# Two hybrid layers on one core: modulation vectors from feature-major weights, and a first stage built around them

## The chip, the cores and the metric

The kernel runs on one core of one Trainium2 chip. The metric is the device time of one execution in microseconds (us). Five engines work in parallel, each through its own list of instructions: TensorE (PE in the profile, its weight loads PEld), VectorE (DVE), ScalarE (ACT), GpSimd (POOL) and SyncE (SP), which here issues the transfers (DMAs) from device memory.

## The reference

256 tokens of width 1024 pass two layers. In each, the condition vector c makes six vectors of 1024, which shift, scale and gate the activations. Cut to this:

```python
def rmsnorm(x, g):
    return x * lax.rsqrt(jnp.mean(x * x, axis=-1, keepdims=True) + EPS) * g

mod = c_act @ ada_w + ada_b                  # c_act = silu(c), ada_w 1024 x 6144
sh1, sc1, gt1, sh2, sc2, gt2 = [m[:, None, :] for m in jnp.split(mod, 6, axis=-1)]

h = rmsnorm(x, mix_pre_g) * (1.0 + sc1) + sh1
proj = h @ w_in                              # 1024 x 10272: z, xbc, dt, sc_b, sc_c, sc_h, gates
...                                          # Mamba-2 scan, short convolution, gates -> mix
x = x + gt1 * rmsnorm(mix, mix_post_g)
h = rmsnorm(x, ffn_pre_g) * (1.0 + sc2) + sh2
u = causal_dwconv(h @ w_up, ffn_conv_w, ffn_conv_b)
u_gate, u_val = jnp.split(u, 2, axis=-1)
f = (jax.nn.silu(u_gate) * u_val) @ w_down
x = x + gt2 * rmsnorm(f, ffn_post_g)
```

The second layer has attention (sparse and latent) in place of the scan and its own condition vector and weights `w_ada_2`; its six vectors are called sha, sca, ga (around the attention) and shf, scf, gf (around its feed-forward part).

## The kernel before, in words

**The stream.** All weights are fp32 and are read once, some 230 MB. They come as half chunks of at most 128 x 1024 into six buffers `raw`. ACT makes `hi` of a half chunk (a rounded copy in the format that TensorE multiplies), VectorE makes `lo` = raw - hi, five buffers each. An activation is split the same way (`hh` and `hl` for h, `h3h` and `h3l` for h3, and so on), and a product is three: hi by xh, lo by xh, hi by xl. `cast_next` takes the next half chunk of the list `keys` and issues its cast and difference; u16 means half chunk number 16 of the list. The first 16 (`w0`, 128x768 and 128x800 for each slice) belong to the first stage, u16 to u23 to the z part of `w_in`.

**The order.** Everything is put in order when the program is built. `_Order` keeps a clock for each engine and a rank for each task (tasks are generators); `O.spawn` starts one, `O.drain` runs one to its end. SP issues the transfers in the order of `keys`. Every engine operation is issued in one helper, so all have line 401 in the profile; transfers have their own lines (510 `raw`, 784 `ada0`, 435 a row broadcast over the partitions).

**The modulation vectors.** gt1, gt2, ga and gf are wanted as rows (1024 values, the same in all partitions), the other six as columns (128 features in the partitions, 8 columns). Their weights come with 128 of the 1024 inputs in the partitions. `ada_mul` lets VectorE multiply each half chunk by a column of silu(c) (`cact`) and add it into one accumulator `adaacc`; `ada_task` then has TensorE sum it over the partitions against `ones`: eight products of width 1 for a column vector, two of width 512 (`row_sum`) for a row. `mix_in` puts these chunks between the others in `keys`. gt2, shf and gf go another way (`adp_load`, `adp_add`, `adp_fill`, `adp_end`): buffers of their own, 6 or 7 of their 8 parts on VectorE (`ND`), the rest as products of width 512 (`adp,cb` and `adp,ones`) in waits of TensorE. shf comes out as a row, and `adp_end` turns it into columns by eight products `ones,row`.

**The first stage.** Of the first layer, h is needed at once. Slice by slice (t = 0 to 7, 128 features each) `mod_acc` accumulates the shift and the scale on VectorE (`ada0acc`), `mod_sum` adds TensorE's part (`cact,ada0a`, and the sum against `ones`) and makes m, `mod_h` makes hf and hh on ACT, `mod_lo` makes hl, and `half(0)` and `half(1)` are the slice's 39 products with w0 (the columns B, C and a quarter of x of the scan's input, and dt). `cast0` casts one half chunk. POOL scales xT by the token's rsqrt for slices 1 to 7. After this stage come z (`z_task`), the rest of x, and so on.

**The tail of gt2.** `tail` is the code between two blocks: it makes the residual, norms it, turns it by products `btok,xr` (four rows of the list, two records each in the trace) and applies shift and scale, which gives h3h and h3l. While h3h is made, TensorE's list holds the products of the `fill` vector, here shf:

```python
    h, k_h, of = tail("gt2", True, "h3", "sca", "sha", "shf")
```

In the second layer the list of keys goes nc, ns, nw (attention's keys and values), then queries, then `wo2`, `up2`, `dn2`.

Of the kernel before, what the change touches and what calls it, by code (L numbers as in the profile page):

```python
# [15 lines left out]
D = 1024  # L16
# [9 lines left out]
           "shf": ("w_ada_2", 3), "scf": ("w_ada_2", 4)}  # L26


def _plan():
# [129 lines left out]
for _key, _n in PF_W.items():  # L159
# [6 lines left out]
         "gq": 256, "gks": 256, "gkw": 256, "mq": 128, "mk": 128}  # L166
# [8 lines left out]
def _rows(i):  # L175
    def swap(v):
# [8 lines left out]
         "mq": swap(i["mla_q_norm_2"][128:]), "mk": swap(i["mla_k_norm_2"][128:])}  # L185
# [221 lines left out]
def _body(ctx: ExitStack, tc: tile.TileContext, wst, pf_d, rows_d, cst_d, xT_d, x_d, w2_d, out_d):  # L407
# [353 lines left out]
    on_pe = ("gt2", "shf", "gf")  # L761
    assert sorted(map(str, keys)) == sorted(str(k) for k, _, _ in PLAN if k[0] != "ada0" and k[1] not in on_pe)
# [35 lines left out]
    AC.activation(cact, P("c", 0, 16), AF.Silu)  # L798
# [18 lines left out]
    def mod_sum(t):  # L817
        a = acc0.pop(t)
        for j in range(2):
            o = adps[:, 2 * t + j:2 * t + j + 1]  # L820
            for k in range(PK[t]):
                PE.matmul(o, ws0(t, k)[:, 128 * j:128 * j + 128], cact[:, k:k + 1], start=k == 0, stop=False)
            PE.matmul(o, a[:, 128 * j:128 * j + 128], ones[:, 0:1], start=PK[t] == 0, stop=True)
        del ada0[t]
        ada0_dma(t + 4)
        m = m01[t] = sm.tile([128, 2], F32, name="m01")
        VE.tensor_add(m, adps[:, 2 * t:2 * t + 2], P("b01", 2 * t, 2))
        VE.scalar_tensor_tensor(m[:, 1:2], m[:, 1:2], 1.0, P("g1", t), op0=OP.add, op1=OP.mult)
# [18 lines left out]
    for _ in range(WARM):  # L847
        PE.matmul(xbc[0][:, :128], ones, ones, start=True, stop=True)
    for q in range(4):
        AC.activation(sq[:, 512 * q:512 * q + 512], xT[:, 512 * q:512 * q + 512], AF.Square)  # L850
        for k in (2 * q, 2 * q + 1):
            for t in range(2):
                PE.matmul(dtps[:, t:t + 1], sq[:, 256 * k + 128 * t:256 * k + 128 * t + 128], ones[:, 0:1], start=k == 0 and t == 0,
                          stop=k == 7, skip_group_check=True)
    r2 = sm.tile([128, 2], F32, name="r2")
    mod_acc(0, 0, SPLIT0)
    rsqrt(r2, dtps[:, :2], D, 1e-6)
    mod_acc(0, SPLIT0, 8)
    for t in range(2):
        PE.matmul(dtps[:, 128 + 128 * t:256 + 128 * t], r2[:, t:t + 1].to_broadcast([128, 128]), ident, start=True, stop=True)  # L860
    if EARLY > 0:
        cast0()
    mod_sum(0)
    rs = fresh1("rs")
    AC.copy(rs, dtps[:, 128:384])
    VE.tensor_mul(xTv[:, 0], xTv[:, 0], dtps[:, 128:384])
    for t in range(1, 8):
        GP.tensor_mul(xTv[:, t], xTv[:, t], rs)
    if EARLY > 1:
        cast0()  # L870
    hf = mod_h(0)
    if EARLY < 1:
        cast0()
    mod_lo(0, hf)
    if EARLY < 2:
        cast0()
    mod_acc(1, 0, 8)
    cast0()
    cast0()
    for t in range(8):  # L880
        w = W(t)

        def half(hf_):
            for f in range(6 * hf_, 6 * hf_ + 6):
                mm3(ab(xbc[f // 2], f % 2), w, f * 128, 128, h.hi(t), h.lo(t), t == 0 and f % 2 == 0, t == 7,
                    skip_group_check=True)
# [6 lines left out]
        mod_acc(t + 2, 0, 4)  # L893
        cast0()
# [8 lines left out]
        cast0()  # L903
        half(1)
# [16 lines left out]
    acc = {}  # L921

    def ada_mul(nm, k, w):
        s = cact[:, (8 if nm in ADA2 else 0) + k:(8 if nm in ADA2 else 0) + k + 1]
        if k == 0:
            if ada_last:
                O.drain(ada_last.pop())
            assert not acc
            a = acc[nm] = wk.tile([128, 1024], F32, name="adaacc", bufs=1)
            VE.tensor_scalar(a, w, s, None, op0=OP.mult)  # L930
        else:
            VE.scalar_tensor_tensor(acc[nm], w, s, acc[nm], op0=OP.mult, op1=OP.add)
# [71 lines left out]
    def adp_end(nm, ps):  # L1004
        p0, p1 = ps
        if nm in ADA_ROW:
            yield from row_sum(nm, [p0, p1])
        else:
            yield from room(a2=2)
            rw = a2("row"), a2("row")  # L1010
            for j in range(2):
                AC.copy(rw[j][:1], ps[j][:1])
            O.cur.onpe = True
            yield
            O.cur.onpe = False
            for f in range(8):
                PE.matmul(p0[:, f:f + 1], rw[f // 4][:1, 128 * (f % 4):128 * (f % 4) + 128], ones[:1, :1], start=True, stop=True)
            O.rel("a2", 2)
            free(p1)
            yield  # L1020
            col_sum(nm, p0)
# [6 lines left out]
    def col_sum(nm, ps):  # L1028
        m = MOD[nm] = const.tile([128, 8], F32, name="mod_" + nm)
        VE.tensor_add(m, ps[:, :8], P("b_" + nm, 0, 8))  # L1030
        free(ps)
        if nm in ("sc2", "sca", "scf"):
# [1423 lines left out]
```

## Time and profile before

| | |
|---|---|
| time, median of 3 runs | 1069.52 us (1068.08 to 1071.35) |
| the profiled execution | 1069.8 us, of which span 1068.0 us |
| busy share PE / DVE / ACT / POOL | 98% / 80% / 59% / 5% |
| mean granted clock of TensorE | 0.992 |
| read from device memory | 229.62 MB, 217 GB/s over the span |

The span runs from the first to the last instruction of the trace; what lies around it is in the time and not in the trace. Busy shares are means over stages that have different limits. The granted clock is TensorE's own: 1.00 stands for 2.4 GHz, 0.50 for 1.2 GHz. A time in brackets behind a row is how long the engine stood idle just before, and who released it.

### The profile page before, as it was taken

Reading aid. Unit: us, or ns where it says so; the run is one execution under the profiler, and the core shown is the slowest. Engines: PE = TensorE matmul, PEld = TensorE weight load, DVE = VectorE, ACT = ScalarE, POOL = GpSimd, SP = SyncE. Lnnn points to the kernel's source line nnn. Section 1 sums busy time; section 2 is a strip of 40 time slices with the busy share of each in tenths; the row PEclk is TensorE's granted clock in tenths of the full one; section 3 lists DMA queues with packets and bytes.
Section 4 is the critical chain, followed back from the end, with each engine's and each line's share of the span. In section 5 each row is a group of like instructions: output and inputs, shape, how many; then the busy total and the mean of one; then the engine's idle time right before and its main releaser. Section 6 shows DMA issues by size and latency. Waiting matters only on the chain.

```text
span 1068.0 us, 19085 instructions
## 1 busy us (share of the span) xinstructions
PE 1042.0 (98%) x7263; PEld 960.9 (90%) x7263; DVE 850.2 (80%) x1502; ACT 625.0 (59%) x1228; POOL 51.7 (5%) x66
## 2 busy tenths in 40 slices
PE   7999999999999999999999999999999889999998
PEld 7899999899999979999988789878999769999986
DVE  5878988987877868898887788898779787878843
ACT  3457569467654356656543666768775446666531
POOL 2000000000100000000000000231110000000000
PEclk8999999999999999999999999999999999999999
DMA  9855577666868856686699377874255836555551
GB/s 352 311 178 174 172 248 252 198 223 229 275 214 292 309 194 220 230 263 208 223 324 346 106 249 253 301 239 143 81 170 190 277 115 208 181 181 181 192 183 40
DMA packets 65902, 233.00 MB, mean 218 GB/s; under 512 B 7537, under 2 KB 8593, under 8 KB 65297
## 3 DMA queue, kind: packets, MB, share of 16 engines
q1 hardware_dynamic: 65808, 231.78, 63.9%
q8 instruction: 57, 0.93, 0.3%
q14 instruction: 37, 0.29, 0.1%
HBM read 229.62 MB, written 2.13 MB: 217 GB/s over the span
## 4 chain that ended last, share of the span: by engine, by line
PE 84%; DVE 6%; DMA 5%; ACT 3%; issue 2%; POOL 1%; SPq 0%; DVEq 0%; ACTq 0%; POOLq 0%
PE ps L401 84%; DVE lo L401 2%; DMA adp<-in_wst_dram 2%; DMA raw<-in_wst_dram 1%; ACT hi L401 1%; DMA ada0a<-in_wst_dram 1%; DVE adp L401 1%; DMA xT<-in_xT_dram 0%; ACT S L401 0%; POOL ssq L401 0%; DVE adaacc L401 0%; DMA brow<-in_rows_dram 0%; DVE S L401 0%; POOL sskv L401 0%; DVE tmp L401 0%
## 5 line engine op out<-in xcount | busy, mean ns | idle before, releaser
L401 DVE TENSOR_TENSOR lo<-raw,hi 128x1024 fp32r<-128x1024 f32 (+3 forms) x326 | 388.5, 1197 | 146.5 <-ACT hi L401 145.0
L401 ACT CAST hi<-raw 128x1024 fp32r<-128x1024 f32 (+3 forms) x326 | 333.3, 1031 | 225.3 <-PE ps L401 194.7
L401 PE MATMUL ps<-hh,hi 128*128 128x256 f32 (+1 forms) x520 | 152.4, 293 | 4.1 <-ACT hh L401 4.1
L401 PE MATMUL ps<-hl,hi 128*128 128x256 f32 (+1 forms) x520 | 148.8, 286 | 0.5 <-DVE hl L401 0.4
L401 PE MATMUL ps<-hh,lo 128*128 128x256 f32 (+1 forms) x520 | 148.6, 286 | 0.0
L401 PEld LDWEIGHTS ps<-hh,hi 128*128 128x128 f32 (+1 forms) x520 | 100.4, 193 | 5.9 <-ACT hh L401 4.5
L401 PE MATMUL ps<-h4h,hi 128*128 128x256 f32 x352 | 99.8, 286 | 2.8 <-ACT h4h L401 2.8
L401 PEld LDWEIGHTS ps<-hl,hi 128*128 128x128 f32 (+1 forms) x520 | 100.4, 193 | 2.4 <-issue 1.2
L401 PEld LDWEIGHTS ps<-hh,lo 128*128 128x128 f32 (+1 forms) x520 | 100.4, 193 | 0.1
L401 PE MATMUL ps<-h4h,lo 128*128 128x256 f32 x352 | 99.7, 286 | 0.0
L401 PE MATMUL ps<-h2h,hi 128*128 128x256 f32 x352 | 98.5, 284 | 0.0
L401 PE MATMUL ps<-h2h,lo 128*128 128x256 f32 x352 | 98.3, 283 | 0.0
L401 PE MATMUL ps<-h2l,hi 128*128 128x256 f32 x352 | 94.7, 283 | 0.0
L401 PE MATMUL ps<-h4l,hi 128*128 128x256 f32 x352 | 94.5, 283 | 0.0
L401 DVE SCALAR_TENSOR_TENSOR fc<-ps,pf,fc 128x254 f32<-128x254 f32 (+1 forms) x176 | 72.3, 474 | 0.0
L401 PEld LDWEIGHTS ps<-h4h,hi 128*128 128x128 f32 x352 | 68.7, 195 | 3.0 <-ACT h4h L401 3.0
L401 PEld LDWEIGHTS ps<-h4h,lo 128*128 128x128 f32 x352 | 68.7, 195 | 0.0
L401 PEld LDWEIGHTS ps<-h2h,hi 128*128 128x128 f32 x352 | 67.6, 192 | 0.8 <-ACT h2h L401 0.8
L401 PEld LDWEIGHTS ps<-h2h,lo 128*128 128x128 f32 x352 | 67.6, 192 | 0.0
L401 PEld LDWEIGHTS ps<-h2l,hi 128*128 128x128 f32 x352 | 65.4, 192 | 0.0
L401 PEld LDWEIGHTS ps<-h4l,hi 128*128 128x128 f32 x352 | 65.4, 192 | 0.0
L401 DVE SCALAR_TENSOR_TENSOR adaacc<-raw,cact,adaacc 128x1024 f32<-128x1024 f32 x49 | 62.7, 1280 | 0.5
(389 smaller groups left out, 2390.7 us busy)
## 6 DMA issues: line engine op xcount, KB each, us to landing
raw<-in_wst_dram SPq DMA_DIRECT2D x356, 512.0 KB, 4.8
adp<-in_wst_dram SPq DMA_DIRECT2D x24, 512.0 KB, 6.8
ada0a<-in_wst_dram SPq DMA_DIRECT2D x8, 512.0 KB, 8.0
ada0b<-in_wst_dram SPq DMA_DIRECT2D x8, 512.0 KB, 8.7
E<-scr SPq DMA_DIRECT2D x4, 1024.0 KB, 7.4
raw<-in_wst_dram SPq DMA_DIRECT2D x8, 400.0 KB, 7.6
raw<-in_wst_dram SPq DMA_DIRECT2D x8, 384.0 KB, 7.4
brow<-in_rows_dram SPq DMA_DIRECT2D x4, 512.0 KB, 7.0
```

Of the source, the lines that this page charges most:

```text
L401: return f(*a, **k)
```

## The change

It has four parts.

1. The weights of all modulation vectors but gt2 and gf are stored the other way round, with features in the partitions and the 1024 inputs along the row. `crow` is silu(c) as a row in every partition. One reduction on VectorE (`tensor_tensor_reduce`: multiply by crow and sum along the row) gives one column of the vector. Column vectors need no product. Row vectors gt1 and ga are spread over the partitions by four products 128x128 for each half (`cst,mod_gt` and `cst,mod_ga`). For the second layer crow is loaded again behind gt1's last reduction, and ACT applies Silu at its first use.
2. shf joins the stream, behind ("ns", 0) and then two chunks apart. The gt2 tail has no fill any more; a task that loads tables (`rot_task`) waits for a flag `rot_go` where it waited for shf's loads.
3. The first stage is written anew: crow is loaded just behind x; the squares are shared by VectorE and ACT; dummy products stand in three places (12, 6 and 8 where there were 20 at the start); each slice takes two reductions; xT is scaled on VectorE; slice 0 has its h made in one step from the rsqrt's bank and its first half ordered by part.
4. In the loop over slices, both halves' products stand first, then the next slice's modulation, then two casts.

```diff
+ON_PE = ("gt2", "gf")
...
-        cols = np.concatenate([np.arange(128) + 128 * t, np.arange(128) + 1024 + 128 * t])
-        plan.append((("ada0", t), 2048, b_list("ada_w", 0, 8, cols)))
+        plan.append((("ada0", t), 2048, lambda i, t=t: np.concatenate([i["ada_w"][:, o + 128 * t:o + 128 * t + 128].T for o in (0, 1024)], 1)))
...
-WARM = 20
-SPLIT0, EARLY = 8, 2
+WARM = (12, 6, 8)
...
-ND = {"gt2": 6, "shf": 7, "gf": 7}
+LAST_C = "gt1"
+ND = {"gt2": 6, "gf": 7}
...
+    mix_in("shf", ("ns", 0), 2)
...
+    crow = wk.tile([128, 1024], F32, name="crow", bufs=1)
+    row_load(crow, "c")
...
+    def mod_dot(t, j):
 
         if t < 8:
-            if k0 == 0:
-                acc0[t] = fresh1("ada0acc")
-                VE.tensor_scalar(acc0[t], ws0(t, PK[t]), cact[:, PK[t]:PK[t] + 1], None, op0=OP.mult)
-            for k in range(max(k0, PK[t] + 1), k1):
-                VE.scalar_tensor_tensor(acc0[t], ws0(t, k), cact[:, k:k + 1], acc0[t], op0=OP.mult, op1=OP.add)
...
+            if t not in m01:
+                m01[t] = sm.tile([128, 2], F32, name="m01")
+            w = ada0[t][j]
+            VE.tensor_tensor_reduce(out=w, in0=w, in1=crow, scale=1.0, scalar=0.0, op0=OP.mult, op1=OP.add,
+                                    accum_out=m01[t][:, j:j + 1])
+            if j == 0:
+                del ada0[t]
+                ada0_dma(t + 4)
...
+    def scale_x(t):
+        if t < 8:
+            VE.tensor_mul(xTv[:, t], xTv[:, t], rs)
...
+    m0 = m01.pop(0)
+    y0 = fresh1("hf")
+    VE.scalar_tensor_tensor(y0, xTv[:, 0], m0[:, 1:2], rs_ps, op0=OP.mult, op1=OP.mult)
+    cast0()
+    AC.activation(h.hi(0), y0, AF.Identity, bias=m0[:, 0:1])
+    VE.scalar_tensor_tensor(h.lo(0), y0, m0[:, 0:1], h.hi(0).bitcast(F32), op0=OP.add, op1=OP.subtract)
...
-        mod_acc(t + 2, 0, 4)
-        cast0()
-        mod_acc(t + 2, 4, 6)
         half(0)
+        half(1)
+        mod_dot(t + 1, 1)
+        mod_dot(t + 1, 0)
+        mod_end(t + 1)
         if t < 7:
-            mod_sum(t + 1)
             hf = mod_h(t + 1)
-        mod_acc(t + 2, 6, 8)
-        if t < 7:
+            cast0()
             mod_lo(t + 1, hf)
-        cast0()
-        half(1)
+            cast0()
+        scale_x(t + 2)
...
-    h, k_h, of = tail("gt2", True, "h3", "sca", "sha", "shf")
+    h, k_h, of = tail("gt2", True, "h3", "sca", "sha", None)
```

How the lists change at three places. First VectorE's list, one slice in the middle of the first stage, before (line numbers are the program's own in each version; a number behind a name tells buffers apart, `m` is the shift and scale of a slice):

```order
L401 SCALAR_TENSOR_TENSOR ada0acc<-ada0b,cact,ada0acc 128x256 x2
L401 TENSOR_TENSOR hl_511<-hf,hh_510 128x256
L401 TENSOR_TENSOR lo<-raw,hi 128x800
L401 TENSOR_SCALAR ada0acc<-ada0a,cact 128x256
L401 SCALAR_TENSOR_TENSOR ada0acc<-ada0a,cact,ada0acc 128x256
L401 TENSOR_TENSOR lo<-raw,hi 128x768
L401 SCALAR_TENSOR_TENSOR ada0acc<-ada0b,cact,ada0acc 128x256 x2
L401 TENSOR_TENSOR m_578<-ps_94,pf 128x2
L401 SCALAR_TENSOR_TENSOR m_578<-m_578,pf 128x1
```

and the same engine and stage after; a reduction appears as two rows `ISA`, the second of which reads out the sum:

```order
L408 TENSOR_TENSOR hl_207<-hf,hh_206 128x256
L408 TENSOR_TENSOR lo<-raw,hi 128x800
L408 TENSOR_TENSOR xT<-xT,rs 128x256
L408 ISA ada0b,m_453<-ada0b,crow 128x1024
L408 ISA m_453 128x1
L408 ISA ada0a,m_453<-ada0a,crow 128x1024
L408 ISA m_453 128x1
L408 TENSOR_TENSOR m_453<-m_453,pf 128x2
L408 SCALAR_TENSOR_TENSOR m_453<-m_453,pf 128x1
L408 TENSOR_TENSOR lo<-raw,hi 128x768
```

What was accumulated two slices ahead in pieces is now one block of the next slice, behind both differences of the slice that is running. Then ACT's list at the end of the first stage (`ta` is the evacuation of dt, `cv` the convolution's first step; casts of 128x1024 are those of the z weights), before:

```order
L401 ACTIVATE hf<-xT,m_715 128x256
L401 CAST hh_510<-hf 128x256
L401 CAST hi<-raw 128x1024 x3
L401 ACTIVATE ta<-ps_93,pf 32x256
L401 CAST hi<-raw 128x1024
L401 ACTIVATE cv<-ps_87,pf 128x256 x2
L401 ACTIVATE cv<-ps_90,pf 128x256 x2
L401 ACTIVATE cv<-ps_88,pf 128x256 x2
L401 CAST hi<-raw 128x1024 x2
```

and after:

```order
L408 ACTIVATE hf<-xT,m_638 128x256
L408 CAST hh_460<-hf 128x256
L408 CAST hi<-raw 128x768
L408 CAST hi<-raw 128x800
L408 ACTIVATE ta<-ps_93,pf 32x256
L408 CAST hi<-raw 128x1024
L408 ACTIVATE cv<-ps_87,pf 128x256 x2
L408 ACTIVATE cv<-ps_90,pf 128x256 x2
L408 CAST hi<-raw 128x1024 x3
```

The casts of 128x1024 ahead of `ta` are gone: the first of them stands behind it. Last, TensorE's list in the tail of gt2, before:

```order
L401 MATMUL ps_91<-btok,xr_4153 128x128 x4
L401 MATMUL ps_93<-btok,xr_4153 128x128 x4
L401 MATMUL ps_87<-adp,cb 128x512
L401 MATMUL ps_92<-adp,cb 128x512
L401 MATMUL ps_87<-adp,ones 128x512
L401 MATMUL ps_92<-adp,ones 128x512
L401 MATMUL ps_94<-hi,h3h_6559 128x512
```

and after:

```order
L408 MATMUL ps_94<-btok,xr_4064 128x128 x4
L408 MATMUL ps_91<-btok,xr_4064 128x128 x4
L408 MATMUL ps_90<-hi,h3h_6430 128x512
L408 MATMUL ps_90<-lo,h3h_6430 128x512
L408 MATMUL ps_90<-hi,h3l_6431 128x512
```

The four products of shf between the turned residual and the first product with h3h are gone.

Counted over the whole lists, 40 products `ones,adaacc` of width 1, 28 `cact,ada0a`, 16 `ones,ada0acc`, 8 `ones,row` and 4 `adaacc,ones` of width 512 leave TensorE, 16 of 128x128 come; VectorE gains 16 reductions in the first stage and 64 behind it.

## Rows read from the trace of the kernel before

**Rows 1.** The page's first part: busy us, share of the span, instructions of each engine.

```profile
PE 1042.0 (98%) x7263; PEld 960.9 (90%) x7263; DVE 850.2 (80%) x1502; ACT 625.0 (59%) x1228; POOL 51.7 (5%) x66
```

**Rows 2.** Chain that ended last: start us, length us, what, number of instructions.

```profile
29.56 335.22 PE ps L401 x2580
...
402.19 204.17 PE ps L401 x1424
```

**Rows 3.** Windows: stretch, length; PE, PEld, DVE, ACT, POOL; clock, DMA share, GB/s.

```profile
30.00:34.00 4.00, 4.00 (x25) 4.00 (x24) 3.33 (x6) 0.54 (x1) 0.00 (x0) 0.60 1.03 412
34.00:72.00 38.00, 38.00 (x323) 37.77 (x323) 28.67 (x57) 17.44 (x26) 0.00 (x0) 1.00 0.68 227
610.00:688.00 78.00, 78.00 (x462) 68.11 (x461) 65.59 (x109) 53.31 (x112) 8.82 (x9) 1.00 0.75 248
688.00:714.00 26.00, 25.58 (x147) 20.63 (x145) 24.67 (x49) 19.67 (x72) 8.14 (x7) 1.00 0.90 311
```

**Rows 4.** Timeline of a first-stage slice: start us, us, engine, operation, [idle before].

```profile
41.02 0.60 ACT L401 ACTIVATE hf<-xT,m 128x256 f32<-128x256 f32 x1 [3.07 <-DVE m L401]
...
41.97 0.86 ACT L401 CAST hi<-raw 128x800 fp32r<-128x800 f32 x1
...
42.09 0.43 DVE L401 TENSOR_TENSOR hl<-hf,hh 128x256 fp32r<-128x256 f32 x1 [0.19 <-ACT hh L401]
...
42.86 0.99 DVE L401 TENSOR_TENSOR lo<-raw,hi 128x800 fp32r<-128x800 f32 x1 [0.34 <-ACT hi L401]
...
48.85 0.99 DVE L401 TENSOR_TENSOR lo<-raw,hi 128x800 fp32r<-128x800 f32 x1 [0.34 <-ACT hi L401]
```

**Rows 5.** Groups of VectorE by shape: busy us, mean ns | idle before.

```profile
L401 DVE TENSOR_TENSOR lo<-raw,hi 128x1024 fp32r<-128x1024 f32 x300 | 364.7, 1221 | 142.4 <-ACT hi L401 140.9
...
L401 DVE SCALAR_TENSOR_TENSOR adaacc<-raw,cact,adaacc 128x1024 f32<-128x1024 f32 x49 | 62.7, 1280 | 0.5
...
L401 DVE CUSTOM_DVE_ANT_0 S<-ps,cst 128x256 f32<-128x256 f32 x16 | 6.0, 418 | 0.0
...
L401 DVE TENSOR_SCALAR adaacc<-raw,cact 128x1024 f32<-128x1024 f32 x7 | 5.2, 746 | 0.0
```

**Rows 6.** Timeline behind the first stage.

```profile
71.70 0.40 PE L401 MATMUL ps<-hi,hh 128*128 128x512 f32 x1
...
80.94 1.20 DVE L401 TENSOR_TENSOR lo<-raw,hi 128x1024 fp32r<-128x1024 f32 x1
...
82.07 2.41 DVE L401 SCALAR_TENSOR_TENSOR cv<-ps,pf,cv 128x255 f32<-128x255 f32 x6
...
84.41 1.20 DVE L401 TENSOR_TENSOR lo<-raw,hi 128x1024 fp32r<-128x1024 f32 x1
...
94.35 1.05 ACT L401 CAST hi<-raw 128x1024 fp32r<-128x1024 f32 x1 [1.82 <-PE ps L401]
```

**Rows 7.** Timeline of the program's start.

```profile
8.52 0.35 DVE L401 TENSOR_SCALAR ada0acc<-ada0a,cact 128x256 f32<-128x256 f32 x1 [8.52 <-DMA ada0a<-in_wst_dram]
...
29.10 0.39 PE L401 MATMUL ps<-hh,hi 128*128 128x256 f32 x1 [2.07 <-ACT hh L401]
```

**Rows 8.** Groups of TensorE by shape; two records stand for one product.

```profile
L401 PE MATMUL ps<-btok,xr 128*128 128x128 f32 x96 | 12.1, 279 | 1.3 <-DVE btok L401 1.3
...
L401 PE MATMUL ps<-ones,adaacc 128*128 128x1 f32 x80 | 9.3, 246 | 0.0
...
L401 PE MATMUL ps<-ones,row 1*128 1x1 f32 x16 | 1.9, 246 | 0.0
...
L401 PE MATMUL ps<-adaacc,ones 128*128 128x512 f32 x8 | 4.1, 593 | 0.0
```

**Rows 9.** Timeline of the tail of `gt2`.

```profile
594.27 1.88 PE L401 MATMUL ps<-adp,cb 128*128 128x512 f32 x4
...
595.99 1.88 PE L401 MATMUL ps<-adp,ones 128*128 128x512 f32 x4
...
596.60 0.64 ACT L401 CAST h3h<-jk 128x512 fp32r<-128x512 f32 x1
```

More of the change, by code (lines that the diff above doesn't have):

```diff
@@ L760, in _body @@
     mix_in("scf", ("q1", 1), 1)
-    on_pe = ("gt2", "shf", "gf")
-    assert sorted(map(str, keys)) == sorted(str(k) for k, _, _ in PLAN if k[0] != "ada0" and k[1] not in on_pe)
+    mix_in("shf", ("ns", 0), 2)
+    assert sorted(map(str, keys)) == sorted(str(k) for k, _, _ in PLAN if k[0] != "ada0" and k[1] not in ON_PE)
     nc.sync.dma_start(pf[:, :PF_HEAD], pf_d[:, :PF_HEAD])
@@ L845, in cast0, with warm @@
         O.cur = None
-    for _ in range(WARM):
-        PE.matmul(xbc[0][:, :128], ones, ones, start=True, stop=True)
+    def warm(n):
+        for _ in range(n):
+            PE.matmul(adps[:, :128], ones, ones, start=True, stop=True)
+    warm(WARM[0])
     for q in range(4):
[L850 to L854, printed above, removed]
+        o, i = sq[:, 512 * q:512 * q + 512], xT[:, 512 * q:512 * q + 512]
+        if q % 2:
+            VE.tensor_mul(o, i, i)
+        else:
+            AC.activation(o, i, AF.Square)
@@ L855, in _body @@
+    AC.activation(crow, crow, AF.Silu)
+    AC.activation(cact, P("c", 0, 16), AF.Silu)
+    for k in range(8):
+        for t in range(2):
+            PE.matmul(dtps[:, t:t + 1], sq[:, 256 * k + 128 * t:256 * k + 128 * t + 128], ones[:, 0:1], start=k == 0 and t == 0,
+                      stop=k == 7, skip_group_check=True)
+    warm(WARM[1])
     r2 = sm.tile([128, 2], F32, name="r2")
-    mod_acc(0, 0, SPLIT0)
     rsqrt(r2, dtps[:, :2], D, 1e-6)
-    mod_acc(0, SPLIT0, 8)
+    mod_dot(0, 1)
@@ L859, in _body @@
+    mod_dot(0, 0)
+    rs_ps = dtps[:, 128:384]
     for t in range(2):
-        PE.matmul(dtps[:, 128 + 128 * t:256 + 128 * t], r2[:, t:t + 1].to_broadcast([128, 128]), ident, start=True, stop=True)
-    if EARLY > 0:
-        cast0()
-    mod_sum(0)
-    rs = fresh1("rs")
[L865 to L869, printed above, removed]
-        cast0()
-    hf = mod_h(0)
@@ L872, in _body @@
[L872 to L877, printed above, removed]
+        PE.matmul(rs_ps[:, 128 * t:128 * t + 128], r2[:, t:t + 1].to_broadcast([128, 128]), ident, start=True, stop=True)
+    warm(WARM[2])
+    mod_end(0)
+    m0 = m01.pop(0)
[4 more added lines that the diff above has]
+    VE.scalar_tensor_tensor(h.lo(0), y0, m0[:, 0:1], h.hi(0).bitcast(F32), op0=OP.add, op1=OP.subtract)
@@ L878, in _body @@
+    rs = fresh1("rs")
+    AC.copy(rs, rs_ps)
     cast0()
-    cast0()
+    scale_x(1)
     for t in range(8):
@@ L883, in half @@
         def half(hf_):
-            for f in range(6 * hf_, 6 * hf_ + 6):
+            if t == 0 and hf_ == 0:
+                for p, (u, x) in enumerate(((0, h.hi(0)), (1, h.hi(0)), (0, h.lo(0)))):
+                    for f in range(6):
+                        PE.matmul(ab(xbc[f // 2], f % 2), w.hi(f * 128, 128, u), x, start=p == 0 and f % 2 == 0,
+                                  stop=False, skip_group_check=True)
+            for f in range(6 * hf_, 6 * hf_ + 6) if t or hf_ else ():
                 mm3(ab(xbc[f // 2], f % 2), w, f * 128, 128, h.hi(t), h.lo(t), t == 0 and f % 2 == 0, t == 7,
@@ L920, in _body, with crow_load @@
     ADA2 = ("sha", "sca", "ga", "shf", "scf", "gf")
-    acc = {}
+    crow_is = ["c", True]
+    def crow_load(c):
+        row_load(crow, c)
+        O.dma(512, O.t["dve"])
+        crow_is[:] = [c, False]
     def ada_mul(nm, k, w):
-        s = cact[:, (8 if nm in ADA2 else 0) + k:(8 if nm in ADA2 else 0) + k + 1]
+        assert crow_is[0] == ("c2" if nm in ADA2 else "c")
+        if not crow_is[1]:
+            AC.activation(crow, crow, AF.Silu)
+            crow_is[1] = True
         if k == 0:
[L926 to L932, printed above, removed]
+            MOD[nm, "c"] = const.tile([128, 8], F32, name="mod_" + nm)
+        VE.tensor_tensor_reduce(out=w, in0=w, in1=crow, scale=1.0, scalar=0.0, op0=OP.mult, op1=OP.add,
+                                accum_out=MOD[nm, "c"][:, k:k + 1])
         if k == 2 and nm in ADA_ROW:
@@ L1004, in adp_end @@
     def adp_end(nm, ps):
[L1005 to L1021, printed above, removed]
+        yield from row_sum(nm, ps)
     def adp(nm, spared):
@@ L1026, in adp, with ada_task @@
         adp_sum[nm] = O.spawn(adp_add(nm))
[L1028 to L1032, printed above, removed]
-            VE.scalar_tensor_tensor(m, m, 1.0, P({"sc2": "g2", "sca": "ga", "scf": "gf"}[nm], 0, 8), op0=OP.add, op1=OP.mult)
-            VE.tensor_scalar(m, m, D ** 0.5, None, op0=OP.mult)
-    def ada_task(nm, a):
-        O.cur.now += 2000
-        if nm not in ADA_ROW:
-            yield
-            ps = yield from tbank()
-            for f in range(8):
-                PE.matmul(ps[:, f:f + 1], a[:, f * 128:f * 128 + 128], ones[:, 0:1], start=True, stop=True)
-            yield
-            col_sum(nm, ps)
-        else:
-            yield from row_sum(nm, [], a)
+    def ada_task(nm, m):
+        if nm in ADA_ROW:
+            O.cur.now += 1000
+            yield from row_sum(nm, [], m)
+        else:
+            VE.tensor_add(m, m, P("b_" + nm, 0, 8))
+            if nm in ("sc2", "sca", "scf"):
+                VE.scalar_tensor_tensor(m, m, 1.0, P({"sc2": "g2", "sca": "ga", "scf": "gf"}[nm], 0, 8), op0=OP.add, op1=OP.mult)
+                VE.tensor_scalar(m, m, D ** 0.5, None, op0=OP.mult)
+            MOD[nm] = m
+            yield
     def row_sum(nm, pss, a=None):
@@ L1057, in row_sum @@
                 ps = yield from tbank()
-                PE.matmul(ps, ones, a[:, s], start=True, stop=True)
+                for f in range(4):
+                    PE.matmul(ps[:, 128 * f:128 * f + 128], a[:, 4 * j + f:4 * j + f + 1].to_broadcast([128, 128]), ident,
+                              start=True, stop=True)
                 yield
```

64 lines of the change are left out of this document (28 added, 36 removed).

## Prediction

> **What bounds the kernel now.** I read the page first. Its first part says that TensorE is busy for 98% of the span [rows 1], so I ask of every edit what it does to TensorE's list. The chain of waits confirms it: one stretch of 335 us and one of 204 us contain nothing but TensorE's products [rows 2]. Two places differ. The windows show that VectorE is almost full at 688–714 (24.67 of 26 us), where TensorE loses a little, while at 610–688 TensorE never stops and VectorE idles for 12.4 of 78 us [rows 3]. The first stage is TensorE's too: at 34–72 it runs 323 products in 38 us, 0.118 us each, without a pause [rows 3]. A slice takes 6.0 us there (the same cast's difference recurs at 42.86 and 48.85) [rows 4]: 51 products, of which 39 are the stage's own and 12 make the shift and scale of the next slice.
>
> **A reduction's price.** The trace has no 128x1024 product that is summed along its row. The nearest row of the same custom kind is 418 ns for 128x256 [rows 5]; a plain two-input operation of 128x1024 takes 1221 ns, a scalar one with an accumulator input 1280, and one with a single input 746 [rows 5]. It reads two inputs, so I take 1.2 us, with 0.75 and 1.3 as bounds. In the stream it replaces operations of 1.28 us one for one, which changes nothing on VectorE.
>
> **The first stage.** Before, it ends at 71.70, where the next products start [rows 6]. After, its start depends on landings. The first `ada0a` was in at 8.52 (the operation that waited for it) [rows 7]. 512 KB at the 412 GB/s of 30–34 [rows 3] take 1.27 us, so with `crow` ahead of it and `ada0b` behind it the first slice's weights are complete at about 11.3. crow itself takes ada0a's old place, about 8.5, and has its table load and Silu by 11, so it doesn't hold. Two reductions end at 13.8, m at 14.25. The rsqrt and its broadcast have no more work ahead of them than before and run beside this, so I let the reductions set it. y0 and h.hi lead to the first real product at 15.4; lo, hl, lo, the scaling and the next two reductions, one behind another on VectorE, bring slice 1's m to 20.5.
>
> From there each slice is one serial round over two engines. Before, sums and weights lay two slices ahead; now the order gives lo(768), hl, lo(800), scaling, two reductions and m on VectorE, and the next hf waits for m. From hf to the end of the cast behind hh is 1.81 us (41.02 to 42.83) [rows 4]; then lo 0.9, hl 0.42, lo 0.95, scaling 0.42 (priced as hl, which has its size), reductions 2.4, the two small operations of m 0.35: 7.25, and 7.1 with the overlaps that such rows show at their joints (80.94 to 84.41 holds 1.20 and 2.41 in 3.47) [rows 6]. TensorE needs 39 x 0.118 = 4.6 us, so it now waits 2.5 us in every slice, in two pieces of about 1.2. m of slice 7 is there at 20.5 + 6 x 7.1 = 63.1; its hl 3.2 later; 38 products behind that 4.5: **70.8, or -0.9**. A gap of 2.07 before 29.10 [rows 7] was followed by a granted clock of 0.60 at 30–34 [rows 3], which is 1.2 GHz for most of these 4 us and cost 4 x 0.40 = 1.6 us. The new gaps are shorter but many; half of one such stretch: +0.8. **Stage: -0.1.**
>
> **Behind it: no casts ahead.** Before, 20 half chunks were cast by the end of the stage, four beyond its own 16; the new loop casts 16. What hid the casts and differences of the z weights was this lead, and it is gone. TensorE's eight units u16 to u23 ran from 71.70 to 94.35 (when the cast that waited for u23's buffer started) [rows 6], without a stop [rows 2]: 2.83 us each. Now ACT first empties dt, casts u16 (1.05 [rows 6]), does four convolution pieces, and casts u17; VectorE's differences end at 2.9 and 5.7 after the stage. Then VectorE alternates six convolution steps with one difference, 3.47 us a round [rows 6], more than 2.83. The difference of u23 ends at 5.7 + 6 x 3.47 = 26.5, ten of its twelve products follow, 2.4: 28.9 against 22.65. **+6.2.** Bounds: 2.9, if only the first wait stays, and 8.0, if each round adds one of ACT's casts.
>
> **What leaves TensorE.** All sums over partitions of width 1 go: 80 records, 9.3 us [rows 8], two to a product, 40 products. sh2 and sc2 are 32 of them in a stretch where TensorE only computes [rows 2]: **-3.7**. sha, 16: **-1.9**. sca lies just ahead of the gt2 tail: -1.8. In that tail TensorE ran shf's last products from 594.27 to about 597.7 while h3h was made, whose first piece is cast at 597.24 (596.60 + 0.64) [rows 9]; without them it waits there, so only 0.4 of the 3.4 us comes back. The 16 turning products of shf, 1.9 [rows 8], stood in TensorE's list a little later: **-4.1 together**. But a gap of 3 us opens, longer than that of 2.07, and half a stretch at 1.2 GHz belongs to it: **+0.8**. scf lies just ahead of the full stretch of VectorE, which takes back part of it: half of 1.9, **-1.0**. gt1 and ga lose 4.1 us of products of 512 and gain 32 records at 12.1/96 each, 4.0 [rows 8]: 0.
>
> **shf on VectorE.** Its eight reductions, 9.6 us, enter at the first attention steps. There 12.4 us are idle and TensorE was the one waited for [rows 3], so they fit: the cover is the lead in casts. What doesn't fit is late in 688–714, where VectorE has 1.3 us left. I take **+0.5**; bounds 0 and 9.6 - 1.3 = 8.3. The operations of shf that ran earlier, up to the gt2 tail, leave VectorE too, where it wasn't the bound: 0. `crow` loaded again is one more 512 KB on a path that had room: 0.
>
> **The sum** is -0.1 + 6.2 - 3.7 - 1.9 - 4.1 + 0.8 - 1.0 + 0.5 = -3.3. The profiled execution took 1069.8 us (span 1068.0 and 1.8 around it), 0.3 above the median of the runs, 1069.52. So 1069.8 - 3.3 = 1066.5, and **1066.2** as a median.
>
> **The rivals.**
> Slower by the clock: with two waits of some 1.2 us in every slice, TensorE is granted half its clock through much of the first stage. For it: the 2.07 gap and the 0.60 behind it. Against: at 34–72 the granted clock stayed at 1.00 although the stage's engines meet each slice. At 1.2 GHz a slice's 39 products take 9.2 us, more than 7.1, so TensorE would set the pace: 7 x 2.1 = 14.7 if all slices are slow, half of it as the likely size: 1066.2 + 7.4 = 1074 (1071 to 1081). It decides from about three slow slices on. The Trainium skill ("TensorE: Matmul & The Clock Gate", section "A second HAM failure mode: psum-queue depth-cycling") says that short idle moments between groups of products, if frequent, make the clock swing between its two levels. By that rule this rival would be the forecast and the time 1074; the trace of before has no such train of gaps, so no row decides it. Chance 0.17.
>
> Slower by shf: VectorE's lead isn't there when 688 comes, and its 9.6 us push the full stretch back by up to 8.3: 1074. For it: 24.67 of 26 us. Against: the idle 12.4 us ahead. It decides once more than 3 of the 9.6 us are late. Chance 0.15.
>
> Faster by cheap reductions: they run at the one-input pace of 0.746 [rows 5]. A slice is then 6.2 us, the stage ends 0.9 + 6 x 0.9 = 6.3 earlier: 1060. Against: two-input operations of that size all took over 1.2. Chance 0.18.
>
> The change not doing what it says is not among them: the new lists show every product of width 1 of these vectors gone.
>
> **How the numbers follow.** The forecast has 0.50. Its own range is 1061 to 1071 (the z term from 2.9 to 8.0, clock terms from none to one full stretch each). The range for 8 in 10 reaches to the centres of the rivals: 1059 to 1075. A measurement tells about 0.3%, 3.2 us, so faster means below 1066.3, and my number stands on that edge. Half of the forecast case (0.24) and all of the cheap one (0.18) are faster: 0.42. Three quarters of the two slower rivals lie above 1072.7, and with the tail of the z term that is 0.26. The rest, 0.32, can't be told from no change.
>
> **What the new profile would show.** Right: reductions of about 1.2 us; slices 7.1 us apart, first stage ended near 71; TensorE with two short waits in every slice at a clock near 1; from there to the end of u23 about 29 us; the gap before h3h about 3 us; 688–714 much as it was. Wrong: a granted clock near 0.5 to 0.8 in 20–70, slices of 6.2 us or 9, no waits in z, or a longer stretch behind 688. What I trust least is the loss in z, since it decides the sign: without it the change would be worth 9 us.

## The result, and the profile after

The changed kernel takes 1076.59 us (median of 8 runs, 1072.09 to 1080.78), the kernel before 1069.08 (8 runs beside them). The ratio is 1.0057, with a 95% interval of 1.004 to 1.0075: slower by 0.4 to 0.75%. The prediction was 1066.2, with 1059 to 1075 as its range, and faster as its likeliest sign. The profiled execution took 1077.97 us (span 1076.2), 8.1 us more in span than the one of before. One execution of a later run (reductions behind the differences) took 1770.75 us at a mean granted clock of 0.695, and the median and ratio given for that run leave it out.

The first part of the page of the changed kernel answers to [rows 1]: TensorE is busy 9 us less in a span 8 us longer, so its waits have grown.

```profile
PE 1032.7 (96%) x7107; PEld 949.1 (88%) x7107; DVE 846.8 (79%) x1557; ACT 625.4 (58%) x1228; POOL 37.3 (3%) x59
```

Where the time went is read best along the stream of weights. Both kernels make the same 326 differences `lo`, in the same order of chunks. The starts of some of them, read from the two timelines, with the shift between them:

```
difference   before    after   shift   what lies between this line and the line above
      144     472.6    474.6    +2.0   first stage, z, sh2, sc2, gt1
      180     575.6    575.8    +0.2   sha
      184     596.1    594.6    -1.4   sca
      216     673.9    676.2    +2.3   tail of gt2, shf, first attention steps
      256     833.6    835.1    +1.5   scf, ga, most of the attention
      264     880.8    888.9    +8.1   end of the attention, tail of ga
      324    1048.4   1056.5    +8.1   feed-forward part of the second layer
```

At 596 us the changed kernel is 1.4 us ahead. It loses 3.7 us in the first attention steps and 6.6 at the attention's end.

The windows of the changed kernel, with the columns of [rows 3]; the first four stretches are the same as there, the last three are where it loses:

```profile
30.00:34.00 4.00, 3.22 (x27) 3.23 (x28) 4.00 (x7) 0.16 (x1) 0.00 (x0) 1.00 1.03 409
34.00:72.00 38.00, 27.57 (x209) 24.76 (x207) 23.34 (x47) 13.61 (x22) 0.00 (x0) 1.00 0.60 205
610.00:688.00 78.00, 75.45 (x442) 65.59 (x441) 70.88 (x122) 50.79 (x103) 8.77 (x9) 0.98 0.85 290
688.00:714.00 26.00, 26.00 (x148) 21.44 (x146) 24.54 (x49) 17.66 (x61) 5.48 (x7) 1.00 0.91 320
584.00:600.00 16.00, 13.14 (x57) 10.29 (x56) 11.56 (x21) 11.82 (x26) 2.42 (x5) 0.90 0.49 162
634.00:648.00 14.00, 11.46 (x64) 9.76 (x63) 13.50 (x30) 10.24 (x29) 2.32 (x2) 0.88 0.77 254
846.00:870.00 24.00, 18.57 (x98) 16.09 (x97) 17.96 (x28) 4.31 (x10) 0.00 (x0) 0.86 0.73 271
```

In the first stage (34–72) TensorE idles for 10.4 of 38 us, yet its granted clock stays at 1.00 in this execution. In the last three it is both idle and slower: at 584–600 the clock of 0.90 costs 16 x 0.10 = 1.6 us; at 634–648 it idles for 2.5 us and the clock of 0.88 costs 14 x 0.12 = 1.7; at 846–870 it idles for 5.4 (before: 2.3, at a clock of 1.00) and the clock costs 24 x 0.14 = 3.4.

The three waits themselves, from TensorE's timeline after (start, length, operation, in brackets the idle time ahead and its releaser):

```profile
595.85 0.50 PE L408 MATMUL ps<-hi,h3h 128*128 128x512 f32 x1 [2.85 <-ACT h3h L408]
...
637.91 0.69 PE L408 MATMUL ps<-cst,ko 128*128 128x128 f32 x2 [2.54 <-DVE ko L408]
...
857.61 0.69 PE L408 MATMUL ps<-cst,Sm 128*128 128x128 f32 x2 [4.77 <-DVE Sm L408]
```

The first is the bare tail of gt2 [rows 9]. What stood ahead of the other two shows in the chain of waits after, pieces of 620 to 636 and of 847 to 857 (start, length, what):

```profile
620.15 6.71 DMA raw<-in_wst_dram
...
627.98 2.27 DVE lo L408 x2
...
632.19 1.61 POOL ssk L408
...
634.45 0.95 ACT hi L408
635.43 1.23 DVE lo L408
...
847.51 8.48 DMA adp<-in_wst_dram
...
856.01 1.28 DVE adp L408
857.29 0.28 DVE Sm L408
```

At 620 the chain waits for a transfer of the stream: shf's eight half chunks, 4 MB, come now in the same stretch (290 GB/s at 610–688 where [rows 3] have 248). Then VectorE and ACT work through what has piled up. At 847 it is one of gf's own transfers, the second of eight, which lands 8.5 us after its issue; VectorE stands at the gf operation that needs it, and the next piece of softmax, for which TensorE waits, is queued behind it. Before, TensorE's longest wait at 834–860 was 1.20 us.

SyncE's timeline tells when gf's transfers were issued, after:

```profile
836.31 7.52 SPq L517 DMA_DIRECT2D raw<-in_wst_dram  x2
843.92 0.38 SPq L978 DMA_DIRECT2D adp<-in_wst_dram  x1
...
847.51 0.38 SPq L978 DMA_DIRECT2D adp<-in_wst_dram  x1
```

and before:

```profile
834.82 2.25 SPq L510 DMA_DIRECT2D raw<-in_wst_dram  x2
837.17 0.38 SPq L957 DMA_DIRECT2D adp<-in_wst_dram  x1
...
843.18 0.33 SPq L957 DMA_DIRECT2D adp<-in_wst_dram  x1
```

The first load of gf stands at the same place of the queue. After, the load of the stream ahead of it waited for a buffer 5 us longer, so gf's first came 6.7 us later and the second, the one waited for, 4.3, though the kernel as a whole was 1.5 late.

### The profile page after: what moved, and what is told of

It reads as the page before. It is cut to its first block, busy times and chain, and to the rows that moved or that the text cites. A ratio compares the mean times of both kernels' runs of the same rounds, so it can differ in the third digit from the quotient of the medians.

```text
span 1076.2 us, 18740 instructions
## 1 busy us (share of the span) xinstructions
PE 1032.7 (96%) x7107; PEld 949.1 (88%) x7107; DVE 846.8 (79%) x1557; ACT 625.4 (58%) x1228; POOL 37.3 (3%) x59
## 4 chain that ended last, share of the span: by engine, by line
PE 51%; DVE 5%; ACT 4%; DMA 3%; issue 1%; POOL 0%; DVEq 0%; ACTq 0%; POOLq 0%
PE ps L408 51%; DMA raw<-in_wst_dram 2%; DVE lo L408 2%; ACT hi L408 1%; DMA adp<-in_wst_dram 1%; ACT S L408 1%; DVE S L408 0%; ACT jk L408 0%; ACT junk L408 0%; DVE jk L408 0%; DVE raw L408 0%; DVE Sm L408 0%; DVE ropet L408 0%; DVE tmp L408 0%; ACT tmp L408 0%
## 5 line engine op out<-in xcount | busy, mean ns | idle before, releaser
L408 DVE CUSTOM_DVE_ANT_0 raw<-raw,crow 128x1024 f32<-128x1024 f32 x64 | 76.8, 1219 | 0.0
```

Of the source, the lines that this page charges most:

```text
L408: return f(*a, **k)
```

## The experiments

All ratios are to the kernel before on the same chip, in its own runs; the changed kernel's is 1.0057. Differences between two edited kernels are differences of their medians. Where they ran on different chips, they are uncertain by about 1 us, since the medians of the kernel before differ there (1069.08 to 1070.33). Shifts and waits are those of one profiled execution of each kernel.

**shf back on TensorE.** The changed kernel with shf's old way restored (buffers of its own, fill of the gt2 tail, turning products).

```diff
-ON_PE = ("gt2", "gf")
+ON_PE = ("gt2", "shf", "gf")
...
-    mix_in("shf", ("ns", 0), 2)
...
-    h, k_h, of = tail("gt2", True, "h3", "sca", "sha", None)
+    h, k_h, of = tail("gt2", True, "h3", "sca", "sha", "shf")
```

> shf goes back to its old way (own buffers, products in the gt2 tail as fill, turned by eight products); all else as in the changed kernel. In the profile of the changed kernel everything up to 594 us is 1.4 us ahead of the kernel before and everything behind 884 us is 8.1 behind, so 9.5 us are lost in between. Theory A, shf's move caused that (the bare tail, VectorE crowded at 610 to 640, and lists laid out later than before): the time falls by 8 to 10, to about 1067. Rival B, the planner laid the attention's lists out anew and the loss is chance of that layout: any time from 1068 to 1080, with waits at other places. Rival C, the first stage and the z weights: no change, 1075 to 1078.

Measured: 1073.23, ratio 1.0028 (1.0014 to 1.0042): 3.4 us back, not 8 to 10. The shift against before stays at -1.6 us from difference 184 to 216, where the changed kernel goes to +2.3: with shf's move undone, the loss in the first attention steps is gone. At the end 4.1 us are still lost (from -2.0 at difference 256 to +2.1 at 264). So Theory A explains the first of the two losses and not the second.

**shf's reductions earlier.** They stay on VectorE and move into the first layer's last weights.

```diff
-    mix_in("shf", ("ns", 0), 2)
+    mix_in("shf", ("dn", 1), 2)
```

> shf's reductions stay on VectorE but stand in the first layer's last weights (behind dn 1, every third chunk) instead of the first attention steps; the gt2 tail stays without fill. Theory A1, VectorE crowded at 610 to 640 is the main part: the gap of 2.5 us at 635 and the half clock behind it are gone, time falls by 4 to 9, to about 1070. Theory A2, the bare tail is the main part: falls by less than 2. Rival B, the layout of the lists: any time from 1068 to 1080.

Measured: 1071.95, ratio 1.0015 (1.0003 to 1.0028): 4.6 us back. Its window at 634–648 is whole:

```profile
634.00:648.00 14.00, 14.00 (x90) 12.62 (x89) 13.15 (x28) 11.44 (x30) 3.50 (x3) 1.00 0.63 205
```

From difference 184 to 216 it gains 2.1 us on before, with the bare tail and its wait of 2.85. So the tail was priced right, and the place of shf's reductions wrong. That this isn't chance of a layout shows in the runs below: in the five with the reductions at the first attention steps (the changed kernel is one of them) the stretch loses 3.7 to 5.3 us, each with a wait of 2.5 to 3.4 ahead of `cst,ko`; in the six with them early it gains 0.5 to 2.1 and that wait is gone. Whether their 9.6 us on VectorE or their 4 MB decided isn't told apart: the edit moves both.

**Reductions behind the differences.** Meant to put a slice's reductions one slice ahead:

```diff
     scale_x(1)
+    mod_dot(1, 1)
+    mod_dot(1, 0)
+    mod_end(1)
...
-        mod_dot(t + 1, 1)
-        mod_dot(t + 1, 0)
-        mod_end(t + 1)
         if t < 7:
...
         scale_x(t + 2)
+        mod_dot(t + 2, 1)
+        mod_dot(t + 2, 0)
+        mod_end(t + 2)
```

> The reductions of a slice stand one slice further ahead (behind the differences of the slice before, two slices before their use), so hf no longer waits for them; the lists of TensorE behind the first stage are the same. If a slice was the serial round of 7.1 us: VectorE's 5.5 to 5.6 us set the pace, six slices give 9 us back, some of it eaten in the z weights: 1067 to 1070. Rival, the transfers of the modulation weights hold the reductions: 1072 to 1075. Rival, a slice is limited by something else: no change.

Measured: 1076.55, ratio 1.0054 (1.0037 to 1.0071): nothing. The edit doesn't do what its expectation says. It turns the loop's body without changing the order around it: the reductions still stand between one slice's last difference and the next slice's hf, and ACT's hf still waits 4.52 us for m, as in the changed kernel.

**The planner's slack.** Nothing computed changes.

```diff
-PHASE = ((2500.0, 5, 1800.0), (2000.0, 5, 1800.0), (2500.0, 3, 1800.0), (3000.0, 3, 2100.0))
+PHASE = ((2500.0, 5, 1800.0), (2000.0, 5, 1800.0), (2400.0, 3, 1800.0), (3000.0, 3, 2100.0))
```

> Only the planner's slack in the attention phase is 2400 in place of 2500: nothing is computed otherwise, the lists of the attention are laid out a little differently. Theory A (the loss in the attention belongs to shf's move): within 3 us of the changed kernel. Rival B (it is the chance of a layout): moves by more than 3 us either way, with gaps of several us at other places than 635, 742 and 853.

Measured: 1081.75, ratio 1.011 (1.0086 to 1.0134): 5 us more. The layout of the attention's lists alone moves the time by about as much as either of the two losses. In its profile the wait ahead of `cst,ko` stays (2.54 us at 637.51), while the later ones stand at other places (2.28 at 760.44, 4.85 at 868.81). So rival B holds in part: a loss of 4 us at one place can't be put down to the change by its place alone, only by an experiment that removes its cause.

**Reductions really a slice ahead.**

```diff
     scale_x(1)
+    mod_dot(1, 1)
+    mod_dot(1, 0)
+    mod_end(1)
...
-        mod_dot(t + 1, 1)
-        mod_dot(t + 1, 0)
-        mod_end(t + 1)
+        mod_dot(t + 2, 1)
+        mod_dot(t + 2, 0)
+        mod_end(t + 2)
         if t < 7:
```

> In the run before, the reductions were moved behind the differences but stayed between one slice's differences and the next slice's hf: the same round, only turned, and nothing moved. Here they stand ahead of the running slice's differences and work for the slice after, so hf finds its m a whole round early. If a slice was one serial round over ACT and VectorE: VectorE's own 5.5 us set the pace in place of 7.05, six slices give 9 us: 1067 to 1069. Rival, the transfers (a slice's 1.8 MB take 4.5 us at 410 GB/s) or the split buffers hold it: 3 us or less.

Measured: 1067.03, ratio 0.9964 (0.9951 to 0.9976): 9.6 us less than the changed kernel (9.9 by the ratios), faster than before. Two starts of the same difference, and the m of a later slice between them, from VectorE's timeline:

```profile
39.82 0.96 DVE L408 TENSOR_TENSOR lo<-raw,hi 128x768 fp32r<-128x768 f32 x1
...
43.41 1.22 DVE L408 CUSTOM_DVE_ANT_0 ada0a<-ada0a,crow 128x1024 f32<-128x1024 f32 x1
...
44.87 0.16 DVE L408 SCALAR_TENSOR_TENSOR m<-m,pf 128x1 f32<-128x1 f32 x1
44.98 0.96 DVE L408 TENSOR_TENSOR lo<-raw,hi 128x768 fp32r<-128x768 f32 x1
```

A slice takes 5.16 us and VectorE never waits in it. The serial round is shown.

**Four casts ahead of z**, the reductions as in the change.

```diff
         scale_x(t + 2)
+        for _ in range({6: 1, 7: 3}.get(t, 0)):
+            cast0()
```

> Four half chunks of z are cast ahead at the end of the first stage again (one in slice 6, three in slice 7), as in the kernel before; the reductions stand as in the change. Theory, the missing lead cost 6.2 us: the z weights end about 6 us earlier, and since the planner's lists behind it change too, the whole lands at 1069 to 1073. Rival, TensorE would have waited in z anyway: less than 2 us gained there.

Measured: 1072.45, ratio 1.0006 (0.9993 to 1.0019): 4.1 us less than the changed kernel (5.5 by the ratios). TensorE is busy for all 28 us of 72–100, where the changed kernel has 25.83 at a clock of 0.94:

```profile
72.00:100.00 28.00, 28.00 (x192) 25.89 (x191) 26.87 (x53) 17.66 (x31) 0.00 (x0) 1.00 0.61 206
```

The missing lead is shown as the cause; of the 6.2 us predicted for it, 4.1 to 5.5 came back.

**gf's loads one place earlier**, on top of shf early.

```diff
-    adp("gf", 2)
+    adp("gf", 0)
```

> As the run with shf's reductions in the first layer, and gf's own loads may start with two free buffers fewer, so that the first stands one load of the stream earlier in SyncE's list. Theory, the gap of 2.7 to 4.8 us before the last wo2 products (VectorE stands at a gf operation whose transfer is late, TensorE's next softmax piece is queued behind it) is a matter of when these loads are issued: the gap shrinks, 2 to 4 us less than the run with shf early, 1068 to 1070. Rival, the order of the attention's lists: the gap comes at another place, no gain.

Measured: 1078.19, ratio 1.0071 (1.0059 to 1.0084): 6 us worse than shf early. The expectation failed. A gf operation on VectorE waits 2.94 us for its transfer as late as 854.16, and the window is the worst of all:

```profile
846.00:870.00 24.00, 18.18 (x73) 14.36 (x74) 15.16 (x26) 3.06 (x7) 0.13 (x1) 0.72 0.47 168
```

By SyncE's timeline the first load of gf was issued 10 us earlier than in shf early (831.53 against 841.63). But VectorE's list now has the fourth gf operation at 854.16, where shf early has its third at 855.13, and `osl`, for which TensorE waits 3.28 us at 856.43, stands behind it. Loads of gf and of the stream alternate in one queue: the second of gf, issued at 838.70, stands behind one of the stream at 838.28.

**The edits together**, with that of gf's loads.

> The edits together: reductions a slice ahead, four casts ahead, shf in the first layer, gf's loads earlier. If the terms add (9 + 6 + 4.6 + 3) the time is about 1054; if the first stage's gain and the casts ahead overlap, 1058 to 1062; if the attention's layout decides, anything up to 1072.

Measured: 1063.0, ratio 0.9926 (0.9913 to 0.9938). The shift goes from -18.1 at difference 256 to -8.3 at 264: gf's edit costs its share here too.

**The edits together, without it.**

> The run with the edits together, without the one for gf's loads, which cost 6 us by itself in the run where it stood alone against shf early (the stretch from the 260th to the 264th half chunk went from +0.4 to +6.3 against before). If it does the same here: 1063 - 6 = 1057. If the layout decides: 1057 to 1066.

Measured: 1057.82, ratio 0.9892 (0.9876 to 0.9909). Against the changed kernel that is 18.8 us; the three edits alone gave 9.6, 4.1 and 4.6, in sum 18.3. By the ratios it is 17.6 against a sum of 19.9. They add, within what such differences tell.

**The same with shf on TensorE.**

> Reductions a slice ahead and four casts ahead, shf on its old way through TensorE in the gt2 tail. Against the run with shf early it keeps 12 products and 16 turning records, and has no bare tail. If the two ways of shf are worth the same, as the runs that changed only that say (1073.2 and 1072.0): 1057 to 1060.

Measured: 1060.28, ratio 0.9912 (0.99 to 0.9924). shf's two ways are within 2.5 us of each other once VectorE's is well placed.

**gf in the stream**, on top of shf early: no gf operation and no gf transfer apart from the stream at the attention's end.

```diff
-ON_PE = ("gt2", "gf")
+ON_PE = ("gt2",)
...
+    mix_in("gf", ("up2", 4), 2)
...
-    h4, k_h4, of = tail("ga", False, "h4", "scf", "shf", "gf")
-    adp("gf", 2)
+    h4, k_h4, of = tail("ga", False, "h4", "scf", "shf", None)
```

> As the run with shf early, with gf in the stream too (behind up2 4, two chunks apart; feature-major, spread by products as gt1 and ga; the ga tail has no fill). No gf operation stands on VectorE and no gf transfer is on the way at the end of the attention. Theory, VectorE's waits for gf's late transfers make the loss of 3.6 to 4 us at 834 to 880: the gap before the last softmax pieces is gone and the stretch gives 4 us back, less up to 4 for the bare tail: 1068 to 1072. Rival, the loss is the order of the attention's own work: the gap stays with another releaser.

Measured: 1069.06, ratio 0.9996 (0.9982 to 1.0009): 2.9 us less than shf early (2.0 by the ratios, whose intervals overlap). From TensorE's timelines, first the wait in shf early, then this run:

```profile
853.26 0.44 PE L408 MATMUL ps<-cst,Sm 128*128 128x128 f32 x2 [2.72 <-DVE Sm L408]
...
850.05 0.44 PE L408 MATMUL ps<-cst,Sm 128*128 128x128 f32 x2 [0.82 <-DVE Sm L408]
...
868.39 1.01 PE L408 MATMUL ps<-btok,xr 128*128 128x128 f32 x3 [3.40 <-DVE btok L408]
```

From difference 256 to 264 it loses 0.3 us on before where shf early lost 3.6; read at TensorE's first product with `h4h`, behind the ga tail, it is 0.9 against 3.6, since the bare tail takes some of it back. Another 1.7 us go in the feed-forward part, where the products that spread gf now stand.

**All of it, with gf in the stream.**

> Reductions a slice ahead, four casts ahead, shf early, gf in the stream. If the gains add: 1053 to 1057. If the bare ga tail costs what the fill hid: 1057 to 1061.

Measured: 1056.53, ratio 0.9879 (0.9865 to 0.9893), the lowest median, though the interval overlaps that of the same without gf's edit. It beats the kernel before by 1.2% and the changed one by some 20 us (19 by the ratios). The wait ahead of `cst,Sm` answers to gf's edit here too; the three edits without it, then with it:

```profile
835.98 0.44 PE L408 MATMUL ps<-cst,Sm 128*128 128x128 f32 x2 [2.75 <-DVE Sm L408]
...
833.84 0.44 PE L408 MATMUL ps<-cst,Sm 128*128 128x128 f32 x2 [0.83 <-DVE Sm L408]
```

Up to the first product with `h4h` the stretch from difference 256 loses 3.8 us without it, and gains 0.5 with it. Two bases with different lists agree, so gf's own way, its late transfers ahead of the softmax on VectorE, is shown as the cause of the 3 to 4 us that these kernels lose there.

## Why the prediction was wrong, step by step

**What held.** A reduction takes 1.22 us (1.2 predicted), the group of 64 in the page after:

```profile
L408 DVE CUSTOM_DVE_ANT_0 raw<-raw,crow 128x1024 f32<-128x1024 f32 x64 | 76.8, 1219 | 0.0
```

That ends the rival of cheap reductions. The slice is a serial round of 7.05 us (7.1 predicted), as VectorE's timeline after shows, to be read against [rows 4]:

```profile
43.54 0.96 DVE L408 TENSOR_TENSOR lo<-raw,hi 128x768 fp32r<-128x768 f32 x1 [1.84 <-ACT hi L408]
...
47.13 1.22 DVE L408 CUSTOM_DVE_ANT_0 ada0a<-ada0a,crow 128x1024 f32<-128x1024 f32 x1
...
50.59 0.96 DVE L408 TENSOR_TENSOR lo<-raw,hi 128x768 fp32r<-128x768 f32 x1 [1.84 <-ACT hi L408]
```

The first stage ends at 70.86 (70.8 predicted before the clock, whose +0.8 didn't come in this execution). Behind it ACT and VectorE's lists do what the sum assumed, rows that answer to [rows 6]:

```profile
72.35 0.50 PE L408 MATMUL ps<-hi,hh 128*128 128x512 f32 x1 [1.49 <-ACT hi L408]
...
75.08 1.23 DVE L408 TENSOR_TENSOR lo<-raw,hi 128x1024 fp32r<-128x1024 f32 x1 [1.52 <-ACT hi L408]
76.22 2.42 DVE L408 SCALAR_TENSOR_TENSOR cv<-ps,pf,cv 128x255 f32<-128x255 f32 x6
78.56 1.22 DVE L408 TENSOR_TENSOR lo<-raw,hi 128x1024 fp32r<-128x1024 f32 x1
```

The difference of u17 ends 5.45 after the stage (5.7 predicted), the rounds are 3.48 (3.47), u23's begins at 95.92 and ends 26.3 after (26.5). Stage, z, sh2 and sc2 together: +2.0 in the table of shifts, where the terms -0.1, +6.2 and -3.7 give +2.4. sha: -1.8 (predicted -1.9). sca: -1.6 (-1.8). scf with the rest up to difference 256: -0.8 (-1.0). This last one is luck in part, for the stretch holds a loss that no term foresaw; before and after:

```profile
738.00:750.00 12.00, 10.07 (x63) 8.26 (x62) 9.25 (x32) 10.63 (x39) 3.30 (x3) 1.00 0.67 228
738.00:750.00 12.00, 8.98 (x43) 7.04 (x41) 9.50 (x41) 8.74 (x33) 2.28 (x3) 0.73 0.48 159
```

The clock of 0.73 costs 12 x 0.27 = 3.2 us, and by the table of shifts the rest of the stretch makes that up.

In span the forecast was -3.3 and the measurement +8.1. Of the 11.4 us between them, 4.7 are the first attention steps (-1.0 forecast, +3.7 measured) and 6.6 the attention's end (nothing forecast); the other stretches fit within 0.4 each.

**The step that failed first: "they fit: the cover is the lead in casts".** shf on VectorE was put at +0.5, from 12.4 us of VectorE's idle time in 78. From difference 184 to 216 the kernel should have gained about 1 (-0.4 and -1.9 of the tail, +0.8 and +0.5); it lost 3.7. The runs put in its place: without the reductions there, the same stretch gains 2.1 (shf early), so they cost 5.8 less what the clock behind the tail's wait took, 16 x 0.10 = 1.6 in this execution alone: about 4. That is 2.54 us of wait for ko and the 1.7 of the clock behind it. The idle time was a mean over 78 us, but six of the eight reductions, 7.3 us, fall between 610.8 and 633.2. The windows there, before and after:

```profile
612.00:636.00 24.00, 24.00 (x111) 19.91 (x110) 19.09 (x31) 14.76 (x32) 1.44 (x2) 1.00 0.70 243
612.00:636.00 24.00, 23.36 (x107) 18.99 (x105) 22.92 (x40) 12.96 (x31) 2.89 (x2) 1.00 0.95 350
```

Only 4.9 of the 12.4 idle us lay where they came, and 1.1 are left. And the transfers that came with them were not counted at all: "one more 512 KB on a path that had room" speaks of crow and forgets shf's own 4 MB. The rival of shf was right in sign and wrong in place: 688–714 went through unhurt, with 26.00 us busy.

**The step that was missing: gf.** The sum has no term behind scf. The attention's end was taken as it was, and there the largest loss lies, 6.6 us by the table. Some 3 of it are gf's late transfers, as gf in the stream shows on two bases (2.7 and 4.3 us by the first product with `h4h`). The kernels that keep gf's own way as the change has it lose 3.6 to 6.6 there, the changed one most; in its profiled execution the 24 x 0.14 = 3.4 us of lost clock, which stand with the wait, are part of it. What made the transfers late is only read from rows. The load ahead of gf's waits for a buffer that a cast and its difference free, and on ACT this cast stands behind a block of softmax, which waited for VectorE; ACT's timeline after:

```profile
837.00 0.40 ACT L408 ACTIVATE Sm<-Sm,mxm 128x128 f32<-128x128 f32 x1 [2.88 <-DVE mxm L408]
...
841.16 2.00 ACT L408 CAST hi<-raw 128x1024 fp32r<-128x1024 f32 x2
```

Which part of the change laid those lists out so isn't settled. It isn't shf's move, the order of the loop or the missing lead by itself: with each of these undone alone, 4.1, 5.0 and 3.9 us are still lost. The run with another slack moved the whole by 5 us with no change in the work.

**The rival of the clock in the first stage** did not happen in the profiled execution: two waits of about 0.9 us stand in every slice (1.2 foreseen), and the granted clock is 1.00 at 30–34 and 34–72. That was luck in part. Five other runs have the same VectorE and ACT lists up to the z weights and the same train of waits. The one with another slack has 1.00 at 34–72 too; four are lower, with 0.96 (shf back on TensorE; gf's loads earlier), 0.91 (shf early) and 0.87 (gf in the stream):

```profile
34.00:72.00 38.00, 30.84 (x204) 28.55 (x203) 22.86 (x44) 12.80 (x21) 0.00 (x0) 0.87 0.58 204
```

The rule of the Trainium skill ("TensorE: Matmul & The Clock Gate", section "A second HAM failure mode: psum-queue depth-cycling"), that frequent short idle moments make the clock swing, agrees with these four traces in part, and not with that of the changed kernel. What the rival had wrong is the price. It put the likely cost at 7.4 us; in gf in the stream 38 x 0.13 = 4.9 us of clock are lost and the slices stay 7.05 apart, as a slice's waits shrink (one of 0.62 where there were two of 0.9). Only the end shows it: from the last slice's first difference to that of u16 it takes 9.00 us, against 7.63 in the changed kernel, so 1.4 us.

**The order of the loop** was priced right but taken as given: a slice ahead gives 9.6 us, four casts 4.1. Both were in the prediction's own working as the two losses of the first part.

## What to carry to other kernels

When work moves to another engine, count its transfers with it, and look for its cover in the stretch where it lands, operation by operation, not in a mean over a longer one. A reduction that feeds the next step belongs a step ahead of it in an in-order list: moving three lines gave 9.6 us, and turning the loop without changing the order around the dependency gave nothing. Where a planner lays out the lists, a change of 0.5% can be the layout's: move one of its constants first, to see how far the time goes by itself, and put a loss down to a cause only when removing the cause removes the loss, best in two kernels whose lists differ. One profile shows the clock of one execution: read it in several before saying that a row of short waits costs nothing.

## What was not expected of the hardware

The same wait of 2.85 us ahead of h3h was followed by a lower clock in some profiled executions and not in others. The changed kernel has 0.90 at 584–600 (above), 1.6 us lost; shf early, with the same wait and the same lists around it, none:

```profile
584.00:604.00 20.00, 17.15 (x82) 13.79 (x81) 15.49 (x28) 13.05 (x29) 2.42 (x5) 1.00 0.52 177
```

It isn't the kernel alone that decides: gf in the stream has the same lists there as shf early, and 0.79 over the 8 us behind the wait. In the run with the reductions behind the differences it is 0.62 over 8 us, 3.0 us lost. So a wait of that length had a price of 0, about 1.6 or 3.0 us.

The spread of the changed kernel's runs, 1072.09 to 1080.78, is wider than that of the kernel before (1068.08 to 1074.87), and it goes with the granted clock: its two fastest executions have a mean of 0.988 and 0.990, the other six 0.982 to 0.985. Of gf in the stream, the four fastest (1066.56 to 1067.63) have 0.989 to 0.992 and the four slowest (1070.82 to 1073.78) 0.977 to 0.982. Which waits bring that about is not shown.
